# Head-by-head routing of an expert layer: matmul fill moved behind the last head, six mask instructions merged into one, and the row gathers spread

## The chip, the cores and the metric

The kernel runs on one core of a Trainium2 chip. A core has five engines with their own instruction streams: TensorE (PE, matmuls), VectorE (DVE), ScalarE (ACT), GpSimd (POOL) and SyncE (SP, which here only issues DMAs). They meet through semaphores. The metric is device microseconds (us) of one execution, as the median of several runs.

## The reference

One layer of a streaming encoder on 512 tokens of width 1024, in float32. A mixing part (spatial gating and banded attention) is followed by PEER, a layer of 16384 experts, and the change is in PEER's routing:

```
q = (xb @ w_query).reshape(128, 8 heads, 2, 128)
sc = einsum('thpd,hpkd->thpk', q, sub_keys)            # 128 scores for each of the two halves
s_top, i_top = top_k(sc, 16)
cand = s_top[:, :, 0, :, None] + s_top[:, :, 1, None, :]   # 256 sums for each head
best, pos = top_k(cand, 16);  eidx = cand_idx at pos;  g = softmax(best)
h = gelu(einsum('thkd,td->thk', expert_u[eidx], xb))
out = einsum('thkd,thk->td', expert_v[eidx], g * h)
```

So each token chooses 16 experts in each of 8 heads, takes the dot product of its row with 128 rows of `expert_u`, and sums 128 weighted rows of `expert_v`.

## The kernel before

**Dense instead of gathered.** For most tokens the kernel does not gather expert rows. It multiplies all 16384 rows of `expert_u` with the tokens ("first products", 128 tiles of 128 experts, line 553 applies the gelu), builds a matrix of gates from one-hot factors ("one-hot stage", lines 763 to 790), multiplies the two, and multiplies the result with all of `expert_v` ("second product", line 970). Every matmul runs three times on operands split into a high and a low part: `load_split` (lines 119 to 133) loads a tile into one of 3 buffers `raw`, ACT writes `hi` (line 126) and DVE or POOL writes `lo` (line 127), into 5 buffers each. A first-product tile is 24 matmuls into one of two PSUM buffers `pu`, and line 553 on ACT must have read a buffer before the tile after the next may begin.

Two groups of tokens are not dense. Tile 0 (128 tokens) is gathered completely, in the second product's shadow. For the last 64 tokens of tile 3 the dots with `expert_u` are gathered "early": 64 gathers of 128 rows each (two of a token's sixteen experts of a head lie on two partitions, so a head needs 8 gathers), into 6 buffers `rowe`. `indices_early(h)` (lines 501, 502) copies the indices of head h into the tile `eui` on POOL, `gather_early` (line 486) issues indirect DMAs on POOL, `dots_early` (line 495) takes the dots on DVE.

**Routing.** The part of the program from about 225 to 460 us goes head by head. `candidates(h)` splits the head's query weights on POOL, multiplies (48 matmuls into `pa`), copies the result on ACT (line 651, `qt`), multiplies with the keys (line 659), copies the scores (line 662, `scr`) and finds the 16 best keys of each half on DVE (lines 568 to 572). Between these stand first-product tiles as fill for PE: `FILL` tiles in each head, two (`BC`) before head 0, and eight (`BRIDGE`) behind the last head. One iteration later `pairs` adds the keys' scores to 50 candidates (lines 589 to 599) and `choose` takes the 16 best and finds their expert numbers: ACT copies a `tree` (line 606), six bit tests on DVE make masks (line 613), six predicated copies (line 623) select, and line 625 writes `eidx`. I call this the choice of head h, counted from 0 to 7. In each iteration from the third, `indices_early`, then up to six gathers, are queued behind a split on POOL.

After the last choice `indices_of` (lines 677 to 681) makes the digits of the expert numbers, PE transposes them (lines 742, 743), and the one-hot stage begins: 48 steps of 16 small matmuls (line 780), each with a tile `bm` from POOL (line 764) and `am` from DVE (line 772), a quarter of a first-product tile as fill, and gathers for the 64 tokens in the first 33 steps.

**What sets the order.** In routing a list scheduler of the framework decides the order of instructions on each engine from priorities and its own estimates; in the one-hot stage PE, DVE, ACT and POOL follow the order in which the code is written. `tc.issue_after(x)` queues a block's instructions behind x on x's engine. Each engine works through its queue in that order, so an instruction that waits holds all that stand behind it.

## Time and profile before

| | |
|---|---|
| median of three runs | 1463.06 us (1460.8 to 1463.57) |
| the profiled execution: its time, its span | 1460.14 us, 1458.1 us |
| mean granted TensorE clock | 0.986 |
| busy: PEld, ACT, POOL | 1234.7, 615.6, 694.5 us |
| DMA | 396.77 MB, mean 272 GB/s |
| chain that ended last | PE 48%, DVE 9%, DMA 6%, issue 3% |

The page's chain of waits covers the whole program, and the change touches a part of it, so the readings below are of stages: busy time of each engine in a window, and then the instructions that ended PE's idle time. In a row of the timeline the columns are start, duration, engine, line, operation, written tile <- read tiles, shape and count, and in brackets the engine's idle time before it and what ended that. Starts are microseconds from the start of the span.

### The profile page before, as it was taken

The page shows a single profiled execution, that of the slowest core. Times are in us where ns is not written, and L with a number is a line of the kernel's source. Part 1 is how long each engine was busy: PE and PEld are TensorE (multiplying, and loading weights), DVE is VectorE, ACT ScalarE, POOL GpSimd, SP SyncE. Part 2 cuts the span into 40 slices and gives each one's busy share as a digit, 9 for nine tenths or more (in the row PEclk, how much of TensorE's full clock was granted, in tenths as well). Part 3 has the DMA queues.
Part 4 walks back from the last instruction along what each step waited for, and adds up shares of the span by engine and source line. Part 5 has one row for each costly group of instructions (what it writes and reads, how often), then busy time and mean ns, then how long its engine had stood idle before and what let it go on. Part 6 is the DMA issues. An engine that isn't in the chain of part 4 may idle for free.

```text
span 1458.1 us, 21675 instructions
## 1 busy us (share of the span) xinstructions
PE 1397.6 (96%) x7808; PEld 1234.7 (85%) x7808; DVE 1131.7 (78%) x2487; ACT 615.6 (42%) x991; POOL 694.5 (48%) x470
## 2 busy tenths in 40 slices
PE   7999899999988888989999999999999999999998
PEld 5887588888888888979988889989899898888887
DVE  4437643588987887579999999898989889588883
ACT  5447625434344444544444434333433343333331
POOL 0000006478767988605544556555546455244520
PEclk9999999999989999999999999999999999999999
DMA  5352036378656999879889999999999999789981
GB/s 187 116 188 73 17 143 201 110 247 304 219 206 217 296 297 270 259 246 357 309 310 344 328 374 345 359 357 369 384 363 352 361 330 374 273 308 353 332 334 72
DMA packets 164251, 396.77 MB, mean 272 GB/s; under 512 B 12672, under 2 KB 75024, under 8 KB 162096
## 3 DMA queue, kind: packets, MB, share of 16 engines
q1 hardware_dynamic: 65344, 196.76, 37.9%
q0 software_dynamic: 47536, 171.37, 31.9%
q10 hardware_dynamic: 51264, 27.27, 6.4%
q8 instruction: 61, 1.00, 0.3%
q14 instruction: 46, 0.38, 0.1%
HBM read 363.86 MB, written 31.46 MB: 271 GB/s over the span
## 4 chain that ended last, share of the span: by engine, by line
PE 48%; DVE 9%; DMA 6%; issue 3%; ACT 1%; POOL 1%; ACTq 0%; DVEq 0%; POOLq 0%; SPq 0%
PE pa L970 19%; PE px L970 10%; PE pu L144 5%; PE pu L145 5%; PE pu L146 5%; PE pa L780 4%; DVE lo L127 2%; DVE row L911 2%; DMA gd<-gst 2%; DMA sc<-s0d 1%; DMA row<-in_ud,eint 1%; DMA raw<-in_vd 1%; POOL bm L764 1%; DVE acc L922 1%; ACT hi L126 0%
## 5 line engine op out<-in xcount | busy, mean ns | idle before, releaser
L126 ACT ACTIVATE hi<-raw 128x1024 fp32r<-128x1024 f32 x300 | 316.7, 1058 | 469.5 <-DMA raw<-in_vd 137.0
L127 DVE TENSOR_TENSOR lo<-raw,hi 128x1024 fp32r<-128x1024 f32 x248 | 305.1, 1230 | 107.1 <-ACT hi L126 106.0
L909 POOL DMA_INDIRECT row<-in_ud,eint x128 | 201.5, 1574 | 177.8 <-DVE acc L922 121.6
L920 POOL DMA_INDIRECT row<-in_vd,eint x128 | 181.3, 1416 | 172.5 <-DVE row L911 115.6
L144 PE MATMUL pu<-xch,hi 128*128 128x320 f32 x784 | 246.7, 315 | 4.4 <-ACT act L553 4.1
L146 PE MATMUL pu<-xch,lo 128*128 128x320 f32 x784 | 241.3, 308 | 0.3 <-DVE lo L127 0.3
L145 PE MATMUL pu<-xcl,hi 128*128 128x320 f32 x784 | 241.5, 308 | 0.0
L970 PE MATMUL pa<-hi,wh 128*128 128x512 f32 x512 | 200.2, 391 | 0.0
L970 PE MATMUL pa<-lo,wh 128*128 128x512 f32 x512 | 199.6, 390 | 0.0
L127 POOL TENSOR_TENSOR lo<-raw,hi 128x1024 fp32r<-128x1024 f32 x52 | 126.2, 2439 | 88.4 <-ACT hi L126 87.7
L922 DVE SCALAR_TENSOR_TENSOR acc<-row,hw,acc 128x1024 f32<-128x1024 f32 x128 | 164.8, 1288 | 1.2 <-DMA row<-in_vd,eint 1.0
L911 DVE SCALAR_TENSOR_TENSOR row<-row,xb 128x1024 f32<-128x1024 f32 x128 | 157.4, 1232 | 3.9 <-DMA row<-in_ud,eint 3.9
L970 PE MATMUL pa<-hi,wl 128*128 128x512 f32 x512 | 158.3, 389 | 0.0
L144 PEld LDWEIGHTS pu<-xch,hi 128*128 128x128 f32 x784 | 147.6, 188 | 8.4 <-ACT act L553 7.0
L145 PEld LDWEIGHTS pu<-xcl,hi 128*128 128x128 f32 x784 | 147.4, 188 | 1.4
L146 PEld LDWEIGHTS pu<-xch,lo 128*128 128x128 f32 x784 | 147.3, 188 | 0.6 <-DVE lo L127 0.6
L780 PE MATMUL pa<-bm,am 128*128 128x128 f32 x768 | 101.4, 288 | 19.4 <-DVE am L772 11.2
L780 PEld LDWEIGHTS pa<-bm,am 128*128 128x128 f32 x768 | 96.7, 202 | 23.2 <-issue 15.3
L970 PEld LDWEIGHTS pa<-hi,wh 128*128 128x128 f32 x512 | 96.4, 188 | 20.4
L970 PEld LDWEIGHTS pa<-lo,wh 128*128 128x128 f32 x512 | 96.4, 188 | 20.3
L970 PEld LDWEIGHTS pa<-hi,wl 128*128 128x128 f32 x512 | 96.1, 188 | 20.4
L970 PE MATMUL px<-hi,wh 128*128 128x512 f32 x256 | 100.5, 393 | 3.7 <-ACT hi L126 3.7
(215 smaller groups left out, 2618.7 us busy)
## 6 DMA issues: line engine op xcount, KB each, us to landing
raw<-in_uT SPq DMA_DIRECT2D x128, 512.0 KB, 5.6
raw<-in_vd SPq DMA_DIRECT2D x128, 512.0 KB, 5.7
gd<-gst ACTq DMA_DIRECT2D x24, 1024.0 KB, 7.4
gc<-gd SPq DMA_DIRECT2D x15, 1280.0 KB, 8.5
raw<-in_w_in SPq DMA_DIRECT2D x20, 512.0 KB, 4.9
raw<-in_wq SPq DMA_DIRECT2D x16, 512.0 KB, 3.7
raw<-in_w_out SPq DMA_DIRECT2D x8, 512.0 KB, 4.2
gc<-gd SPq DMA_DIRECT2D x15, 256.0 KB, 10.9
```

What stands on the lines that cost most here:

```text
L126: nc.scalar.activation(hi, raw, AF.Copy)
L127: ins = eng.tensor_tensor(lo, raw, hi.bitcast(F32), op=ALU.subtract)
L144: nc.tensor.matmul(ps, lh[0], rh[0], start=first, stop=False)
L145: nc.tensor.matmul(ps, lh[0], rh[1], start=False, stop=False)
L146: nc.tensor.matmul(ps, lh[1], rh[0], start=False, stop=last)
L764: nc.gpsimd.tensor_tensor(bm.rearrange("p t (h l) -> p t h l", l=BL), d[0][:, ts_, :, None].to_broadcast(full), d[1][:, ts_, None, :].to_b ...
L780: nc.tensor.matmul(ps[:, i * P:(i + 1) * P], am[:, 4 * q + i, :], bm[:, 4 * q + i, :], start=True, stop=True)
L909: nc.gpsimd.indirect_dma_start(out=row, out_offset=None, in_=ud, in_offset=bass.IndirectOffsetOnAxis(ap=eint[:, j:j + 1], axis=0))
L911: nc.vector.scalar_tensor_tensor(row, row, 1.0, xb0, op0=ALU.mult, op1=ALU.mult, accum_out=hw[:, j:j + 1])
L920: nc.gpsimd.indirect_dma_start(out=row, out_offset=None, in_=vd, in_offset=bass.IndirectOffsetOnAxis(ap=eint[:, j:j + 1], axis=0))
L922: nc.vector.scalar_tensor_tensor(acc0, row, hw[:, j:j + 1], acc0, op0=ALU.mult, op1=ALU.add)
L970: nc.tensor.matmul(accs[t][half], (wh, wh, wl)[k][:, b, tok], w[b][k % 2][:, ds_], start=first and k == 0, stop=last and k == 2)
```

## The change

- `START` takes the place of `BC` ahead of head 0: one first-product tile where there were two. `FILL` goes from (2, 2, 2, 2, 3, 3, 3, 3) to (1, 1, 1, 3, 3, 3, 3, 3), and `BRIDGE` from 8 to 11. The sum of all three stays 30 tiles. In head 0 the scores stand ahead of the fill tile.
- Six bit tests with a constant become one `tensor_tensor` against a small tile `bits` of six powers of two, over 6 x 48 elements in routing and 6 x 16 where tile 0 is routed later.
- The six gathers of the last head's iteration go: instead one gather follows each of the first six splits of the bridge. `dots_early` is no longer called at the start of the bridge; it is called after the last choice in the code. The index copies for head 6 move from the bridge to behind the last choice, beside those for head 7.
- So 36 gathers are issued by the bridge's end where there were 42, and the one-hot stage asks for a gather in 5 of 6 steps where it was 4 of 6.

```diff
-BRIDGE = 8
+BRIDGE = 11
-FILL = (2, 2, 2, 2, 3, 3, 3, 3)
+START = 1
+FILL = (1, 1, 1, 3, 3, 3, 3, 3)
...
+        bits = const.tile([P, 6], U32, name="bits")
+        for i in range(6):
+            nc.gpsimd.memset(bits[:, i:i + 1], 1 << i)
...
-            for i in range(6):
-                nc.vector.tensor_scalar(mask[:, i * n * TOPK:(i + 1) * n * TOPK], bpos.rearrange("p t k -> p (t k)"),
-                                        1 << i, None, op0=ALU.bitwise_and)
+            full = [P, 6, n * TOPK]
+            nc.vector.tensor_tensor(mask.rearrange("p (l k) -> p l k", l=6),
+                                    bpos.rearrange("p t k -> p (t k)")[:, None, :].to_broadcast(full),
+                                    bits[:, :, None].to_broadcast(full), op=ALU.bitwise_and)
...
-            fill = first_products(sum(FILL[:h]) + BC, FILL[h], nc.gpsimd, True)
-            next(fill, None)
+            fill = first_products(sum(FILL[:h]) + START, FILL[h], nc.gpsimd, True)
+            if h:
+                next(fill, None)
...
         for h in range(NH + 1):
-            dots_early(0)
             if h < NH:
+                dots_early(0)
                 cands.append(candidates(h))
             else:
-                for i, _ in enumerate(first_products(sum(FILL) + BC, BRIDGE, nc.gpsimd, True)):
+                for i, _ in enumerate(first_products(sum(FILL) + START, BRIDGE, nc.gpsimd, True)):
                     behind.append(done[0])
-            if h > 1:
+                    if i < EARLY:
+                        with tc.issue_after(splits[0]):
+                            gather_early(1, gat, ROWA)
+            if 1 < h < NH:
                 with tc.issue_after(splits[0]):
                     indices_early(h - 2)
                     ready_early(h - 2)
-                    gather_early(EARLY, gat, ROWA)
+                    if h < NH - 1:
+                        gather_early(EARLY, gat, ROWA)
...
-        indices_early(NH - 1)
-        ready_early(NH - 1)
+        for h in range(NH - 2, NH):
+            indices_early(h)
+            ready_early(h)
         dots_early(0)
...
-                if n < own - 7 and n % 3 < 2:
+                if n < own - 7 and n % 6 < 5:
                     gather_early(1, gat, ROWA)
```

The rows below show where the instructions stand on their engines, first before and then now. The changed kernel's lines lie 4 to 11 further down the file, so that line 495 is 499 there, and 623 is 628. The first place is DVE at the end of the choice of head 5 (the `eidx` row), before:

```order
L495 SCALAR_TENSOR_TENSOR rowe,du<-rowe,px 128x1024
L623 COPY_PREDICATED tree<-pa,tree 128x48x2
L495 SCALAR_TENSOR_TENSOR rowe,du<-rowe,px 128x1024
L623 COPY_PREDICATED tree<-pa,tree 128x48
L495 SCALAR_TENSOR_TENSOR rowe,du<-rowe,px 128x1024
L625 COPY eidx<-tree 128x3x16
L568 MAX top<-scr 128x8 x2
L569 MAX_INDEX pos<-top,scr 128x8
```

and now:

```order
L628 COPY_PREDICATED tree<-pa,tree 128x48x4
L628 COPY_PREDICATED tree<-pa,tree 128x48x2
L628 COPY_PREDICATED tree<-pa,tree 128x48
L630 COPY eidx<-tree 128x3x16
L499 SCALAR_TENSOR_TENSOR rowe,du<-rowe,px 128x1024
L572 MAX top<-scr 128x8 x2
L573 MAX_INDEX pos<-top,scr 128x8
```

The six dots that stood inside the choice of head 5 are gone from it, and the first dot of the bridge's six gathers stands behind it, ahead of the best keys of head 7. Of the other five, all stand inside the choice of head 6.

The second place is POOL's queue from the index copy for head 4 to the bridge, before:

```order
L501 DMA eui<-eidx 64x8
L502 CAST eui<-eidx 64x8
L127 TENSOR_TENSOR lo<-raw,hi 128x1024 x2
L486 DMA rowe<-in_ud,eui 128x1024 x6
L127 TENSOR_TENSOR lo<-raw,hi 128x1024 x3
L501 DMA eui<-eidx 64x8
L502 CAST eui<-eidx 64x8
L127 TENSOR_TENSOR lo<-raw,hi 128x1024 x5
```

and now:

```order
L505 DMA eui<-eidx 64x8
L506 CAST eui<-eidx 64x8
L131 TENSOR_TENSOR lo<-raw,hi 128x1024 x2
L505 DMA eui<-eidx 64x8
L506 CAST eui<-eidx 64x8
L131 TENSOR_TENSOR lo<-raw,hi 128x1024
L490 DMA rowe<-in_ud,eui 128x1024
L131 TENSOR_TENSOR lo<-raw,hi 128x1024
L490 DMA rowe<-in_ud,eui 128x1024
```

The index copies are for heads 4 and 5. The burst of six gathers between them is gone, and the copy for head 5 stands two splits behind that for head 4. The split behind it is the bridge's first, and the first of the six gathers follows that split.

The third place is DVE in the last choice, before:

```order
L631 TENSOR_TENSOR ex<-gate 128x384
L613 TENSOR_SCALAR pa<-bpos 128x48 x3
L495 SCALAR_TENSOR_TENSOR rowe,du<-rowe,px 128x1024
L613 TENSOR_SCALAR pa<-bpos 128x48 x2
L495 SCALAR_TENSOR_TENSOR rowe,du<-rowe,px 128x1024
L613 TENSOR_SCALAR pa<-bpos 128x48
L623 COPY_PREDICATED tree<-pa,cand 128x48x18
```

and now:

```order
L636 TENSOR_TENSOR ex<-gate 128x384
L617 TENSOR_TENSOR pa<-bpos,bits 128x288
L628 COPY_PREDICATED tree<-pa,cand 128x48x18
L628 COPY_PREDICATED tree<-pa,tree 128x48x16
L628 COPY_PREDICATED tree<-pa,tree 128x48x8
```

No dot stands in the last choice any more.

More of the change, by code (lines that the diff above doesn't have):

```diff
@@ L682, in indices_of @@
             return ff
-        for _ in first_products(0, BC, nc.vector, True):
+        for _ in first_products(0, START, nc.vector, True):
             pass
@@ L713, in hybrid_block @@
         ff = {0: indices_of(GT)}
-        i0 = split = sum(FILL) + BC + BRIDGE
+        i0 = split = sum(FILL) + START + BRIDGE
         def split_next(eng=nc.gpsimd):
```

## The prediction

> **What bounds the kernel now.** I read the page's first part, then the busy times by stage, then what ended PE's idle time in the stage that the change touches.
>
> ```profile
> PE 1397.6 (96%) x7808; PEld 1234.7 (85%) x7808; DVE 1131.7 (78%) x2487; ACT 615.6 (42%) x991; POOL 694.5 (48%) x470
> ```
>
> PE is busy for 96% of the span, and the change leaves the number of matmuls as it is. Only PE's idle time and its clock can be won or lost. The stages below are the first heads, the later heads, bridge and last choice, the gathering part of the one-hot stage, and the second product; the columns are span, PE, PEld, DVE, ACT and POOL busy, then granted clock, DMA share and GB/s.
>
> ```profile
> 225.00:285.00 60.00, 59.20 (x327) 53.38 (x328) 24.43 (x143) 26.87 (x46) 34.42 (x14) 0.97 0.52 163
> 285.00:413.00 128.00, 125.06 (x730) 113.85 (x728) 116.93 (x534) 52.10 (x97) 98.69 (x72) 1.00 0.73 256
> 413.00:466.00 53.00, 42.62 (x257) 41.87 (x258) 39.93 (x167) 21.44 (x32) 34.12 (x25) 0.90 0.54 181
> 466.00:570.00 104.00, 91.18 (x689) 88.08 (x689) 84.70 (x107) 44.21 (x78) 93.58 (x57) 0.95 0.96 294
> 625.00:1458.00 833.00, 823.78 (x4320) 728.73 (x4320) 713.50 (x1246) 326.56 (x469) 393.25 (x265) 1.00 0.88 328
> ```
>
> DVE is idle for 36 of the first 60 us and then busy for 117 of 128: it starts late and runs behind. PE pays at the end, with 10.4 us of idle time in the 53 us of bridge and last choice, and a clock of 0.90. The second product has PE at 99%, so the mask saving there is worth nothing. PE's rows with idle time from the bridge to the first one-hot product:
>
> ```profile
> 415.75 0.63 PE L144 MATMUL pu<-xbh,hi 128*128 128x320 f32 x1 [2.79 <-ACT act L553]
> 424.68 0.41 PE L144 MATMUL pu<-xbh,hi 128*128 128x320 f32 x1 [2.35 <-ACT act L553]
> 457.76 0.55 PE L742 MATMUL pa<-ident,ii 128*128 128x128 f32 x3 [3.13 <-ACT ii L681]
> 465.85 3.30 PE L780 MATMUL pa<-bm,am 128*128 128x128 f32 x16 [2.15 <-issue]
> ```
>
> ACT and DVE show what held the two `act`:
>
> ```profile
> 414.31 1.06 ACT L126 ACTIVATE hi<-raw 128x1024 fp32r<-128x1024 f32 x1 [6.88 <-DMA raw<-in_uT]
> 422.81 1.48 ACT L606 COPY tree<-cand 128x1536 f32<-128x1536 f32 x1 [7.12 <-DVE cand L599]
> 421.75 0.25 DVE L599 TENSOR_TENSOR cand<-top,pa 128x96 f32<-128x96 f32 x1
> 443.89 1.22 DVE L495 SCALAR_TENSOR_TENSOR rowe<-rowe,px 128x1024 f32<-128x1024 f32 x1 [3.99 <-DMA rowe<-in_ud,eui]
> ```
>
> The first `act` stood behind a `hi` whose tile came late. The second stood behind the `tree` copy of head 6, which waited for DVE's candidates. The third gap is the last choice, in which DVE waited 3.99 us for a gather. So DVE's progress through the choices sets the bridge.
>
> **The change part by part.** I take the choice of head 5 (its `eidx` row) as the mark, since the order after it stays the same up to PE's restart.
>
> First the fill. A tile's time is the distance from the first of its 24 matmuls to the next block, and a head's query product that of its 48:
>
> ```profile
> 236.70 0.39 PE L144 MATMUL pa<-xbh,hi 128*128 128x512 f32 x1
> 247.60 0.30 PE L144 MATMUL pu<-xbh,hi 128*128 128x320 f32 x1
> 251.12 1.95 PE L659 MATMUL pa<-skt,qt 128*128 128x128 f32 x16
> ```
>
> A tile is 3.5 us and a query product 10.9. Ahead of the scores of head 1 stood five tiles and now stand three; two tiles are 7.0 us, and I take 6.5, as the scores of head 0 now follow their query product with only four matmuls between and may wait for the copy. Later heads' scores come earlier still (head 3 by four tiles), so PE no longer holds DVE there. What DVE did between the choices:
>
> ```profile
> 272.73 0.49 DVE L568 MAX8 top<-scr 128x8 f32<-128x128 f32 x2 [12.35 <-ACT scr L662]
> 289.19 0.24 DVE L625 COPY eidx<-tree 128x48 f32<-128x48 f32 x1
> 393.77 0.22 DVE L625 COPY eidx<-tree 128x48 f32<-128x48 f32 x1
> 415.05 0.24 DVE L625 COPY eidx<-tree 128x48 f32<-128x48 f32 x1
> 431.71 0.24 DVE L625 COPY eidx<-tree 128x48 f32<-128x48 f32 x1
> L495 DVE SCALAR_TENSOR_TENSOR rowe<-rowe,px 128x1024 f32<-128x1024 f32 x36 | 43.9, 1219 | 6.9 <-DMA rowe<-in_ud,eui 6.5
> L568 DVE MAX8 top<-scr 128x8 f32<-128x128 f32 x36 | 9.9, 282 | 3.0 <-ACT scr L662 3.0
> ```
>
> The `eidx` rows are the choices of heads 0, 4, 5 and 6; the last two rows group 285 to 425 us. From choice 4 to 5 passed 21.3 us with six dots inside, from 5 to 6 16.7 us with none, so a dot costs 0.8 us there (it fills gaps between dependent instructions).
>
> The masks:
>
> ```profile
> L613 DVE TENSOR_SCALAR pa<-bpos 128x48 uint32<-128x48 uint32 x48 | 10.0, 208 | 1.0
> 458.51 0.42 DVE L753 TENSOR_TENSOR hb<-iota_k,pa 128x256 f32<-128x256 f32 x1 [1.35 <-POOL eui L502]
> ```
>
> Six of 208 ns are 1.25 us, with their gaps about 1.45. The merged one has 288 elements, which no row shows; between the 0.42 us of 256 broadcast elements and that of 512 (twice as much) I take 0.45, as it is nearest to the first. It saves 1.0 us a choice (0.6 at worst).
>
> Choice 0 then ends at 289.2 - 6.5 - 1.0 = 281.7. From choice 0 to 5 passed 125.9 us. I take off the 3.0 us wait for scores, the 6.5 us of waits for gathers, five masks (5.0) and seven dots (30 stand there now, 37 before; 5.6), and get 105.8. New waits for gathers come on top. In the changed order POOL's gathers stand in smaller pieces between splits (2.4 us each), and I laid the two queues side by side with the prices of the next fence: 2.0 us in choice 1, 2.7 in choice 3, 2.0 in choice 4, 0.4 elsewhere, 7.1 in all. The bounds are none and the 9.5 that stood there before. Choice 5 falls at 281.7 + 105.8 + 7.1 = 394.6 (387.5 to 397), 20.5 us earlier than now.
>
> Then the new wait. DVE's next instruction is the first dot of the bridge's gathers, and on POOL that gather stands behind the index copy that waits for this very choice, and behind a split:
>
> ```profile
> 415.58 0.56 POOL L501 DMA_DIRECT2D eui<-eidx  x1 [1.09 <-DVE top L568]
> 416.46 2.37 POOL L127 TENSOR_TENSOR lo<-raw,hi 128x1024 fp32r<-128x1024 f32 x1
> DMA to landing us min/median/max: 5.8/5.9/7.1
> ```
>
> From the `eidx` at 415.05 to the end of the copies at 416.46 are 1.4 us, the split is 2.4, and a gather lands 5.9 us after its issue (the third row, of the seven gathers from 430 to 460 us): 9.7, and 1.2 for the dot itself. Thus DVE starts head 7's keys 10.9 us later than it could. Behind the dot stand these keys and the candidates of head 6; for the candidates waits ACT's `tree`, for that the `act` behind it, and for that PE, whose second bridge tile needs the buffer.
>
> The Trainium skill, "DMA: Bandwidth & Descriptors", section "Anatomy of one DMA", gives a GpSimd-issued DMA about 2.0 us and its bytes at 436 GB/s, by which a gather of 512 KB would land after an estimated 3.2 us and the sum would come out 2.7 us lower. The trace says 5.9 and decides.
>
> From the `eidx` of choice 5 to PE's restart passed 424.68 - 415.05 = 9.6 us before. Now PE restarts at 394.6 + 10.9 + 9.6 = 415.1, although its own work would bring it there at about 402. Behind it lie eleven tiles to the transposes (ten of the bridge, one held back) where there were eight: 38.7 us, against 28.2. On the half clock: of the 53 us the clock missed 10%, that is 5.3 us, some of it on the tile ahead of a wait where it cost nothing. 424.68 + 28.2 + 1.7 gives 454.6, which is where the gap at 457.76 begins, so 1.7 was paid behind the restart; after a stall of 13 us I allow 1.7 to 3.4. The transposes come at 455.5 to 457.2. The last choice is over long before, so its 3.1 us of waiting go. Against 457.76 that is a gain of 0.6 to 2.3; I take 1.5.
>
> Last the six gathers, which are not saved but moved into the one-hot stage. POOL's groups from 460 to 570 us, two of PE's rows there, and the gathers' queue and their issues in a view of 480 to 580 us:
>
> ```profile
> L764 POOL TENSOR_TENSOR bm<-hb,lb 128x1024 f32<-128x1024 f32 x34 | 65.5, 1938 | 5.8 <-PE pa L780 3.2 <-DVE lb L753 2.3
> L486 POOL DMA_INDIRECT rowe<-in_ud,eui x21 | 23.3, 1108 | 3.3 <-issue 2.4 <-DVE lb L753 0.2 <-DVE am L772 0.2
> L127 POOL TENSOR_TENSOR lo<-raw,hi 128x1024 fp32r<-128x1024 f32 x4 | 9.6, 2395 | 4.6 <-ACT hi L126 4.6
> 494.32 2.05 PE L780 MATMUL pa<-bm,am 128*128 128x128 f32 x16 [1.41 <-POOL bm L764]
> 503.84 3.65 PE L780 MATMUL pa<-bm,am 128*128 128x128 f32 x16 [3.50 <-DVE am L772]
> q0 software_dynamic: 2639, 9.50, 29.7%
> rowe<-in_ud,eui POOLq DMA_INDIRECT x17, 6.6
> ```
>
> Six gathers of 1.11 us with 0.16 us of issue are 7.6 us more for a POOL that is busy for 93.6 of 104. Its slack, 3.2 us of waiting for PE and 4.6 for `hi`, could swallow them, so the lower bound is nothing. The upper is 10: the 17 gathers issued in those 100 us took 29.7% of the DMA engines, 1.7 us each, while the share stood at 0.96. POOL ends few of PE's gaps (1.41 us), DVE the larger (3.50), so I take 2.5. The six dots more (1.3 us each) lie in DVE's 19 idle us.
>
> The sum is 1460.1 - 1.5 + 2.5 = 1461.1 for the profiled execution. Its runs' median lies 2.9 above it, which gives 1464.0, no change.
>
> **The rivals.** The first is that the gathers hold DVE less than I say. With no wait in choices 1 to 4, choice 5 falls at 387.5 and the transposes 7.1 us earlier: 1456.9. If DVE reached its dot only after the gather had landed, 10.9 us would go, and 1453 is the end of that case. For it speaks that the waits were laid out by hand; against it, that the first gather cannot be issued before choice 5 is over, wherever that falls.
>
> The second ends slower: the one-hot stage pays the gathers in full. POOL becomes the engine that each step waits for once the 7.8 us of its waits are used up, or the DMA engines do at a share that can't rise; the price is 7.6 to 10, and the time 1463.1 - 1.5 + 7.6 to 10, thus 1469 to 1472. For it speaks POOL's 90% and the DMA's 0.96, against it that DVE's waits there leave POOL time.
>
> A third is that the change does all that its description says, the dots behind the last choice, no wait for a gather: 20.5 + 3.1 - 10.5 earlier, 13 us and so 1452 with the gathers' 2.5. The order of DVE speaks against it, so it has little weight and counts with the first.
>
> **How the numbers follow.** About 0.2%, 2.9 us, is what a measurement of this kernel can tell from no change. No change has a chance of 0.37, the first rival with the third 0.33, the second 0.30. The likeliest case's own range is 1460.2 to 1466; to hold eight in ten I go to 1454.5 and 1470.5, into both rivals.
>
> **What would show it.** Right would be: choice 5 at 394 us, a DVE wait of about 9 us for `rowe` right behind it, PE idle for 10 to 13 us in the bridge until 415, and transposes that wait for nothing at 456. Choice 5 after 400, or the transposes before 450, would make the first part wrong. In the one-hot stage, a first product to thirty-third step that takes over 5 us longer would make the second rival right, a length within 1 us my 2.5 too high. PE waiting for `lo` in heads 3 to 7 would mean that POOL, which I take as hidden there, binds.

## The result, and the profile after

The changed kernel takes 1477.6 us (median of four runs, 1474.9 to 1481.9), the kernel before 1461.9 beside it: a ratio of 1.0112 with a 95% interval of 1.0082 to 1.0142. It is slower by 16 us, and 13.6 us above the forecast. The profiled execution took 1474.91 us with a span of 1473.1.

Busy times by stage, first of the kernel before and then of the changed one. The first row of each is routing up to the first one-hot product, the second the one-hot stage up to the first matmul of the second product. The columns are span, PE, PEld, DVE, ACT and POOL busy, granted clock, DMA share and GB/s.

```profile
225.00:465.85 240.85, 226.73 (x1313) 208.95 (x1313) 181.14 (x842) 100.41 (x174) 167.08 (x110) 0.97 0.64 216
465.85:625.27 159.42, 138.42 (x1057) 134.31 (x1057) 118.31 (x150) 72.45 (x126) 127.46 (x78) 0.96 0.92 275
```

```profile
225.00:470.59 245.59, 225.73 (x1307) 207.18 (x1306) 184.13 (x789) 99.79 (x173) 162.70 (x105) 0.97 0.61 200
470.59:641.53 170.94, 141.24 (x1057) 136.46 (x1057) 130.36 (x162) 72.37 (x126) 134.41 (x84) 0.94 0.89 275
```

Routing is 4.7 us longer and the one-hot stage 11.5; the second product, from there to the end of the span, is 1.2 us shorter (831.6 against 832.8). The second rows also say how the 11.5 us are made up: PE's idle time (span less busy) went from 21.0 to 29.7 us, and PE needed 2.8 us more for the same matmuls, at a clock of 0.94 instead of 0.96.

PE's rows with long idle times, of the changed kernel, from the bridge to the second product:

```profile
408.92 0.42 PE L148 MATMUL pu<-xbh,hi 128*128 128x320 f32 x1 [2.75 <-ACT act L557]
420.20 0.63 PE L148 MATMUL pu<-xbh,hi 128*128 128x320 f32 x1 [5.96 <-ACT act L557]
462.55 0.49 PE L753 MATMUL pa<-ident,ii 128*128 128x128 f32 x3
584.95 3.43 PE L791 MATMUL pa<-bm,am 128*128 128x128 f32 x16 [3.39 <-DVE am L783]
595.87 3.76 PE L791 MATMUL pa<-bm,am 128*128 128x128 f32 x16 [4.83 <-DVE am L783]
616.88 2.02 PE L791 MATMUL pa<-bm,am 128*128 128x128 f32 x16 [2.03 <-DVE am L783]
```

The restart in the bridge comes at 420.2 us, five later than forecast, and the transposes (line 753) wait for nothing, as forecast, but at 462.6 instead of 456. The other three rows are in the one-hot stage. They show the clock as well: the same 16 matmuls took 2.02 us behind a wait of 2.03, 3.43 behind 3.39 and 3.76 behind 4.83, and the granted clock in these three stretches was 1.00, 0.57 and 0.50.

On DVE stand the marks of the prediction: the choices of heads 0, 5 and 6, and the first dot behind choice 5. The last row groups all 36 dots from 225 to 470 us.

```profile
281.13 0.23 DVE L630 COPY eidx<-tree 128x48 f32<-128x48 f32 x1
400.10 0.24 DVE L630 COPY eidx<-tree 128x48 f32<-128x48 f32 x1
409.56 1.22 DVE L499 SCALAR_TENSOR_TENSOR rowe<-rowe,px 128x1024 f32<-128x1024 f32 x1 [9.22 <-DMA rowe<-in_ud,eui]
435.26 0.24 DVE L630 COPY eidx<-tree 128x48 f32<-128x48 f32 x1
L499 DVE SCALAR_TENSOR_TENSOR rowe<-rowe,px 128x1024 f32<-128x1024 f32 x36 | 43.7, 1214 | 15.9 <-DMA rowe<-in_ud,eui 15.9
```

Choice 0 is where it was forecast (281.7), choice 5 is 5.5 us late (forecast 394.6). What is late between them is the instruction that was to save time, the merged mask. Its group, two of its rows, and POOL's row beside the first of them:

```profile
L617 DVE TENSOR_TENSOR pa<-bpos,bits 128x288 uint32<-128x288 uint32 x8 | 18.1, 2262 | 0.3
297.85 6.20 DVE L617 TENSOR_TENSOR pa<-bpos,bits 128x288 uint32<-128x288 uint32 x1
324.22 0.46 DVE L617 TENSOR_TENSOR pa<-bpos,bits 128x288 uint32<-128x288 uint32 x1
```

```profile
296.60 7.12 POOL L131 TENSOR_TENSOR lo<-raw,hi 128x1024 fp32r<-128x1024 f32 x3
```

The eight masks of routing took 18.1 us, where 48 bit tests had taken 10.0. Three of the eight took 0.46 to 0.49 us, which is the price that was forecast; the other five took 2.2 to 6.2. The longest began while POOL was in three splits that end at 303.72 and ended at 304.05, 0.33 us behind them. The other four long ones also ended 0.3 us behind the end of one of POOL's splits; the three short ones fell where POOL was issuing gathers (one began 0.2 us before a split's end). Both operands of the mask, `bpos` and `bits`, lie in SBUF (the on-chip memory of the tiles, as against PSUM, the buffers into which PE's matmuls write), and so do both operands of POOL's split. The Trainium skill, "SBUF — State Buffer", section "Who interferes with whom", says that a DVE instruction with two SBUF inputs contends with a GpSimd instruction that reads SBUF; the rows agree, with 0.46 us where POOL had no split and up to 6.20 behind three splits. The bit tests had one SBUF operand and a constant, wrote to PSUM, and never took over 0.213 us.

### The profile page after: what moved, and what is told of

Same layout as the page of the kernel before. It is cut to its first block, busy times and chain, and to the rows that moved or that the text cites. A ratio compares the mean times of both kernels' runs of the same rounds, so it can differ in the third digit from the quotient of the medians.

```text
span 1473.1 us, 21606 instructions
## 1 busy us (share of the span) xinstructions
PE 1399.8 (95%) x7808; PEld 1237.6 (84%) x7808; DVE 1145.0 (78%) x2406; ACT 616.5 (42%) x991; POOL 700.1 (48%) x477
## 4 chain that ended last, share of the span: by engine, by line
PE 54%; DVE 9%; issue 3%; DMA 2%; ACT 1%; POOL 1%; ACTq 0%; DVEq 0%; POOLq 0%
PE pa L981 20%; PE px L981 10%; PE pu L148 6%; PE pu L150 6%; PE pu L149 6%; PE pa L791 4%; DVE lo L131 2%; DVE row L922 2%; DMA gd<-gst 1%; DVE acc L933 1%; DMA sc<-s0d 1%; DVE am L783 1%; POOL bm L775 1%; DMA rowe<-in_ud,eui 1%; DVE ii L685 0%
## 5 line engine op out<-in xcount | busy, mean ns | idle before, releaser
L131 POOL TENSOR_TENSOR lo<-raw,hi 128x1024 fp32r<-128x1024 f32 x53 | 129.3, 2455 | 80.4 <-ACT rstd L156 40.6
```

Of the source, the lines that this page charges most:

```text
L131: ins = eng.tensor_tensor(lo, raw, hi.bitcast(F32), op=ALU.subtract)
```

## Experiments

All ratios below are to the kernel before, run beside on the same chip, with a 95% interval. Stage lengths are those of each kernel's profiled execution, cut as above; where that execution lies far from its kernel's median, the text says so.

**Routing: the mask.** The changed kernel, with the powers of two copied by ACT into six free columns of the mask's PSUM buffer:

```diff
+                powers = ps[:, 8 * ND * TOPK:8 * ND * TOPK + 6].bitcast(U32)
+                nc.scalar.copy(powers, bits)
...
-                                    bits[:, :, None].to_broadcast(full), op=ALU.bitwise_and)
+                                    powers[:, :, None].to_broadcast(full), op=ALU.bitwise_and)
```

> The changed kernel, with one operand of the merged mask moved: ACT copies the six powers of two into six free columns of the PSUM buffer in which the mask lies, and DVE reads them there. Theory: the merged mask (eight times in routing, 2.37 us on the mean, 6.20 us the longest) is long because DVE reads two SBUF tiles in it, and so stands until a split on POOL is over. Then all eight take 0.4 to 0.55 us here, choice 1 ends some 5 us earlier, choice 5 at 391 to 396 us instead of 400.1 (gathers that land late take some of it back), PE restarts in the bridge at 411 to 416, and the run takes 1466 to 1471 us where the changed kernel's profiled run took 1474.9. Rival: 288 elements simply cost that much (or the time is something else's that the profile books here): the eight stay at 2.4 us on the mean and the time within 1 us of the changed kernel's.

(The 2.37 us in it is the median of the eight; the mean is 2.26.) It took 1468.8 us, ratio 1.0051 (1.0032 to 1.0069). The masks of routing, choice 5 and the restart:

```profile
L617 DVE TENSOR_TENSOR pa<-bpos,pa 128x288 uint32<-128x288 uint32 x8 | 3.7, 457 | 0.2
391.99 0.24 DVE L630 COPY eidx<-tree 128x48 f32<-128x48 f32 x1
411.78 0.64 PE L148 MATMUL pu<-xbh,hi 128*128 128x320 f32 x1 [6.96 <-ACT act L557]
```

The same 288 elements cost 0.457 us each with one operand in PSUM. Choice 5 comes 8.1 us earlier, PE's restart 8.4, the first one-hot product 8.6 (462.0). The matmuls, and DVE's order up to choice 4, are those of the changed kernel; ACT has eight small copies more. The rival falls: the length was not the mask's own.

The kernel before with the merged mask alone, both operands in SBUF:

> The kernel before with the merged mask alone, both operands in SBUF (the scheduler moves some gathers and dots with it). Theory of the port: in a choice POOL splits more than half of the time, so the eight masks take 1.5 to 3 us each on the mean where six bit tests took 1.45 with their gaps; the choices come later and the run takes 1464 to 1470 us against 1462. Rival (the prediction's price, 0.45 us each and 1.0 saved in every choice): 1457 to 1462 us.

1467.2 us, ratio 1.0044 (1.0021 to 1.0067): slower, as the theory has it. Its profiled execution lies 14 us above its median, so only the instruction's length is read from it:

```profile
L617 DVE TENSOR_TENSOR pa<-bpos,bits 128x288 uint32<-128x288 uint32 x8 | 15.1, 1888 | 0.3
```

**Routing: the dot behind choice 5.** The changed kernel with the bridge's dots really behind the last choice:

```diff
...
-        dots_early(0)
+        with tc.issue_after(last):
+            dots_early(0)
         routing.close()
```

(`last` is the `eidx` copy that `choose` now returns.)

> The changed kernel, with the dots of the bridge's six gathers queued on DVE behind the last choice, where the code has them and the scheduler did not put them. Theory (the prediction's step on the new wait): the wait of 9.2 us for the first of these gathers, and its dot, hold the keys of head 7, and through them ACT's tree and PE's restart, by 10.9 us. Without them choice 6 comes at 424 to 426 us instead of 435.3, PE restarts at about 410 instead of 420.2, the gaps of 2.75 and 5.96 us shrink by 6 at least, and the run takes 1465 to 1468 us. Rival: something else is as late (ACT's splits, whose tiles land late, or the last choice), PE restarts at 415 or later and the time falls by less than 3 us.

1473.8 us, ratio 1.0074 (1.0048 to 1.0099), some 4 to 6 us better than the changed kernel, though the two intervals overlap. The choices of heads 5 and 6 lie 19.2 us apart instead of 35.2, but PE gained far less. PE's gaps, its routing stage, and what held the first `act`:

```profile
411.57 0.42 PE L148 MATMUL pu<-xbh,hi 128*128 128x320 f32 x1 [1.26 <-ACT act L557]
429.20 0.42 PE L148 MATMUL pu<-xbh,hi 128*128 128x320 f32 x1 [2.11 <-ACT act L557]
225.00:468.17 243.17, 227.71 (x1317) 208.02 (x1317) 187.19 (x790) 100.82 (x174) 164.75 (x105) 0.98 0.61 204
```

```profile
410.13 1.06 ACT L130 ACTIVATE hi<-raw 128x1024 fp32r<-128x1024 f32 x1 [5.70 <-POOL lo L131]
```

Of 8.7 us of gaps 3.4 are left, and PE's idle time from 225 us to the first one-hot product fell from 19.9 to 15.5. From choice 5 to the first product pass 65.5 us instead of 70.5 (the stage as a whole is only 2.4 us shorter, as choice 0 came 2.4 us later in this execution). So the wait of 10.7 us on DVE was worth 4 to 5 us to PE: behind it stand the bridge's tiles, which come from POOL's splits and from loads. The result falls between my two theories.

**The fill alone**, with the six bit tests and the gathers of before:

> The kernel before with the change's fill alone (one tile ahead, fill moved from the first heads behind the last, scores of head 0 ahead of its fill tile), six bit tests, gathers as before. Theory (the prediction's step on the fill): choice 0 ends 6 to 8 us earlier (281 to 283 us), the choices behind it keep most of that, no dot is bound to a gather that waits for choice 5, and the run takes 1456 to 1460 us. Rival: the lead is given back in DVE's waits for gathers and in PE's bridge; the first one-hot product comes at 464 to 467 us as before and the run takes 1460 to 1463.

1456.7 us, ratio 0.9949 (0.9922 to 0.9977): faster. Choice 0 came at 281.48 us and the first one-hot product at 463.4; the one-hot stage took 162.0 us, 2.6 more than before, in an execution that lies 1.4 us above its median, and the second product 2.3 less. So the trace shows 2.5 us gained in routing and given back in the one-hot stage; where the rest of the gain between the runs' medians lies, it does not show.

**The gathers alone** on the kernel before, with old fill and bit tests (of the change's diff, the parts that move the gathers and the index copies and set the pace in the one-hot stage):

> The kernel before with the gathers' part of the change alone: no burst of six in the last head's iteration, one behind each of the bridge's first six splits, 5 of 6 steps in the one-hot stage; six bit tests and the old fill. Theory: most of the one-hot stage's loss comes with it, since the gathers make POOL and DVE late there, and the tail and DVE's instructions with two SBUF operands pay for that: first to last product plus rest 166 to 171 us against 159.4, the routing stage within 3 us of before, the run 1467 to 1475. Rival: the one-hot stage loses by the late start or by the merge, and stays within 2 us of 159.4 here; then the run takes 1460 to 1465.

1474.0 us, ratio 1.0092 (1.0066 to 1.0118). Its one-hot stage, in an execution 7 us below its median:

```profile
465.04:634.64 169.60, 140.77 (x1056) 136.16 (x1057) 129.56 (x162) 72.25 (x126) 134.09 (x84) 0.94 0.90 277
```

10.2 us more than before, and routing within 1 us. So the three parts alone are, by their ratios, worth +13 us (gathers), +6 (merged mask) and -7 (fill), 12 in sum; the whole change is +16 with an interval of 12 to 21.

**The one-hot stage: where its 11.5 us went.** I took the start of the first matmul of each of the 48 steps, counted from the first product. The changed kernel is 2.2 us behind the kernel before at the thirty-third step, 4.2 at the next, 9.0 at the thirty-sixth, and 11.5 from the thirty-seventh to the end. So most is lost where the dots have to be finished. Two rows of DVE and two of POOL of the changed kernel there:

```profile
582.09 1.22 DVE L499 SCALAR_TENSOR_TENSOR rowe<-rowe,px 128x1024 f32<-128x1024 f32 x1 [4.00 <-DMA rowe<-in_ud,eui]
589.84 4.64 DVE L520 TENSOR_TENSOR gate<-gate,dots 64x128 f32<-64x128 f32 x1 [2.52 <-ACT dots L519]
```

```profile
574.20 0.99 POOL L490 DMA_INDIRECT rowe<-in_ud,eui  x1 [0.16 <-issue]
588.61 5.70 POOL L775 TENSOR_TENSOR bm<-hb,lb 128x1024 f32<-128x1024 f32 x3
```

At 5 steps of 6 the last gather is issued at 574.2, one step ahead of the place where all dots are taken, and DVE stands 4.0 us for its rows. Then the early dots are multiplied into the gates, 64 x 128 elements with two SBUF operands; that took 0.79 us before, and 4.64 here, ending 0.17 us behind three of POOL's tiles. Two runs change one of these each. The multiplication from PSUM:

```diff
-                nc.scalar.activation(dots[own], dots[own], AF.Gelu_apprx_tanh)
+                nc.scalar.activation(xbu[own, 0:NH * TOPK], dots[own].rearrange("p a b k -> p (a b k)"), AF.Gelu_apprx_tanh)
```

> The changed kernel, with ACT writing the gelu of the early dots into a PSUM buffer that is free by then, from which DVE multiplies it into the gates (64 x 128 elements). Theory: that multiplication took 4.64 us in the changed kernel and 0.79 before, since both its operands lie in SBUF and POOL wrote three one-hot tiles without a pause. Here it takes 0.3 to 0.5 us, PE's wait of 4.83 us for the next one-hot factor behind it shrinks to about 1, and the time is 1470.5 to 1472 us against 1474.9. Rival: PE waits there for something else that is as late (the copies of the dots and the gelu), and the time stays within 1 us.

1473.1 us, ratio 1.0079 (1.0050 to 1.0107); the stage took 166.8 us, 4.2 less. The stage gained what the theory says, but the run lies just above its range, its interval overlaps that of the changed kernel, and PE now waited longer elsewhere for a one-hot factor (4.58 us at one place). The instruction:

```profile
L520 DVE TENSOR_TENSOR gate<-gate,px 64x128 f32<-64x128 f32 x1 | 0.3, 291 | 2.2 <-ACT px L519 2.2
```

The last gather earlier:

```diff
-                if n < own - 7 and n % 6 < 5:
+                if n < own - 12:
```

> The changed kernel, with the 28 gathers of the one-hot stage issued in its first 28 steps, one in each, instead of in 28 of the first 33. Theory: 10.3 of the stage's 11.5 us were lost from step 33 to 37, of which 4.0 us are DVE waiting for the last gather, which was issued one step ahead of the place where all dots have to be done. Here it is issued five steps earlier: that wait goes, steps 33 to 37 lose about 6 us against the kernel before instead of 10.3, the denser first part costs 1 to 2, and the time is 1471 to 1473 us. Rival (the second of the prediction: the six gathers' time on POOL or on the DMA engines is paid wherever they stand): the first 33 steps get longer by what the end gains, and the time stays within 1 us of 1475.

1478.3 us, ratio 1.0108 (1.0064 to 1.0152), no gain, and the rival's reading is not enough either. The wait of 4.0 us was gone, but two instructions stood behind POOL's tiles for longer than in the changed kernel (rows of DVE and POOL):

```profile
563.63 6.41 DVE L685 TENSOR_SCALAR ii<-ei 128x128 int32<-128x128 int32 x1
592.53 6.05 DVE L520 TENSOR_TENSOR gate<-gate,dots 64x128 f32<-64x128 f32 x1 [1.12 <-ACT dots L519]
```

```profile
564.25 5.69 POOL L775 TENSOR_TENSOR bm<-hb,lb 128x1024 f32<-128x1024 f32 x3
592.73 5.69 POOL L775 TENSOR_TENSOR bm<-hb,lb 128x1024 f32<-128x1024 f32 x3
```

The first is the middle shift of the digits, which has one tensor operand and a target, both in SBUF; it takes 0.2 us when POOL pauses. The same section of the Trainium skill counts `tensor_scalar` among the instructions that can, with suitable operands, use two ports of SBUF and so contend with GpSimd; these rows agree. The kernel before had the same stall, beside two of POOL's tiles and ahead of the wait of 3.50 us for `am` that the prediction shows at 503.84:

```profile
497.91 4.53 DVE L679 TENSOR_SCALAR ii<-ei 128x128 int32<-128x128 int32 x1
498.52 3.81 POOL L764 TENSOR_TENSOR bm<-hb,lb 128x1024 f32<-128x1024 f32 x2
```

So I took all three kinds (masks, gates, digits) off SBUF pairs, that is, gave each an operand in PSUM: the masks and the gates as in the two runs above, the digits by copying the expert numbers into PSUM ahead of the shifts:

```diff
-            ei = gat.tile([P, NH * TOPK], I32, name="ei", tag="ei", bufs=1)
+            ei = pa()[:, 0:NH * TOPK].bitcast(I32)
```

> The changed kernel with the three kinds of DVE instruction that were found long moved off two SBUF operands: the powers of two and the gelu of the dots in PSUM as before, and the copy of the expert numbers from which the digits are shifted in PSUM too. Theory: the digits' second shift took 3.59 us on the mean in the one-hot stage (0.23 for the others) because POOL was writing one-hot tiles, 6 to 7 us in two; with it and the gates' 4.6 gone, the one-hot stage takes 161 to 165 us instead of 170.9, the routing gain of the powers in PSUM (8.6 us) stays, and the run takes 1459 to 1464. Rival (the six gathers' own time on POOL and the DMA engines is the cost): the stage stays above 167 us and the run above 1465.

1462.8 us, ratio 0.9997 (0.9965 to 1.0030): the changed kernel without these stalls is no slower than the one before. The shifts took 0.28 to 0.29 us each. But the stage stayed at 166.0 us, between the theory and its rival. The same with the gathers as before the change:

> The kernel before with the change's fill and merged mask, the three kinds of instruction off two SBUF operands as in the run above, and the gathers as before the change (a burst of six, 4 of 6 steps). Theory: routing gains what the powers in PSUM gave there (first one-hot product at 460 to 463 us instead of 465.9), the one-hot stage 2 to 4 us on top (157 instead of 159.4), and the run takes 1453 to 1458 us, faster than both kernels. Rival: the fill is worth something only together with the gathers spread over the bridge, and the run takes 1459 us or more.

1454.4 us, ratio 0.9967 (0.9945 to 0.9989), faster than both kernels. And the kernel before with the merged mask and the three kinds moved, so without the fill:

> The kernel before with the merged mask and the three kinds of instruction off two SBUF operands, old fill, old gathers: the run of the fill with all that (1454.4 us) less the fill. Theory: the one-hot stage is shorter than before here too (155 to 157 us instead of 159.4), the routing about as before (464 to 466), and the run takes 1456 to 1460. Rival: all of that run's gain came from the fill, and the run takes 1461 us or more.

1456.0 us, ratio 0.9963 (0.9931 to 0.9994), with a first product at 465.2 and a one-hot stage of 154.7 us, as the theory has it: that run's gain did not all come from the fill. With it the first product came 3.1 us earlier, but the two runs' ratios are the same within their intervals.

The runs with all three kinds moved differ in the gathers alone, 166.0 us with the change's and 154.7 with those of before, from first products at 462.20 and 462.18. That is the cost of six gathers moved, 11.3 us in the stage, without the stalls on masks, gates and digits; the runs' medians lie 8.4 us apart. Three runs take it apart. Without six of the 28 dots:

```diff
+        SKIP = (40, 45, 50, 55, 60, 63)
...
                 j, row = issued.pop(0)
+                if j in SKIP:
+                    continue
```

> The changed kernel with the three kinds of instruction off two SBUF operands (1462.8 us, one-hot stage 166.0 us against 154.7 where the gathers are as before), less six of the 28 dots of the one-hot stage, every fifth and the last; their gathers are still issued. It leaves out six of the 64 early rows' dot products. Theory: what the six moved gathers cost is paid on DVE, in dots, their waits and the splits and one-hot factors that stand behind them, so the stage takes 154 to 159 us and the run 1451 to 1456. Rival (the prediction's second): it is paid on POOL and the DMA engines, which here do as much as there; the stage stays at 163 to 166 us and the run at 1460 to 1463.

1463.0 us, ratio 0.9987 (0.9958 to 1.0017), no gain: the rival. (The stage of its profiled execution, 172.0 us, counts little, as that lies 7 us above the median; there one split on DVE stood 5.5 us.) Without the six gathers, all 28 dots kept (six of them on a row that is already there):

```diff
+        SKIP = (40, 45, 50, 55, 60, 63)
...
+                if j in SKIP:
+                    issued.append((j, issued[-1][1]))
+                    continue
                 row = rows_of.tile([P, D], F32, name="rowe", tag="rowe", bufs=n_rows)
```

> The changed kernel off two SBUF operands (1462.8 us, one-hot stage 166.0 us), less six of the one-hot stage's 28 gathers, every fifth and the last; DVE still takes 28 dots, six of them on the row of the dot before. It leaves out six of the 64 early rows' dot products. If POOL's and the DMA engines' time for the gathers is the cost, the stage takes 153 to 158 us; if DVE's dots are, it stays at 163 to 167 us.

1451.8 us, ratio 0.9917 (0.9885 to 0.9949). With POOL's time kept and the transfers dropped:

```diff
-                nc.gpsimd.indirect_dma_start(out=row, out_offset=None, in_=ud,
...
+                if j in SKIP:
+                    nc.gpsimd.memset(row, 0.0)
+                else:
+                    nc.gpsimd.indirect_dma_start(out=row, out_offset=None, in_=ud,
...
```

> The changed kernel off two SBUF operands (one-hot stage 166.0 us; 153.4 without six gathers), with the same six gathers replaced by a memset of the same row tile on POOL (128 x 1024, some 1 us). It leaves out six of the 64 early rows' dot products (they come out as zero). If POOL's time is the cost, the stage takes 162 to 166 us where a memset is as long as a gather's issue (1.11 us), 2 us less for each 0.2 us by which it is shorter. If the transfers are the cost, it takes 153 to 157 us.

1455.0 us, ratio 0.9940 (0.9908 to 0.9971). The one-hot stages of three kernels: 28 gathers, 22 gathers, 22 gathers and six memsets; then the memsets' group.

```profile
462.20:628.21 166.01, 139.61 (x1057) 135.12 (x1057) 124.51 (x162) 72.38 (x126) 133.09 (x84) 0.94 0.92 282
```

```profile
462.30:615.69 153.39, 134.37 (x1057) 129.28 (x1057) 120.59 (x162) 72.84 (x126) 127.91 (x78) 0.98 0.94 285
```

```profile
460.99:617.76 156.77, 136.40 (x1057) 130.85 (x1057) 121.45 (x162) 73.19 (x126) 132.69 (x84) 0.97 0.93 279
L492 POOL MEMSET rowe<- 128x1024 f32 x6 | 5.8, 962 | 0.0
```

Six gathers cost 12.6 us: 7.4 of idle time on PE (26.4 against 19.0), and 5.2 because the same matmuls ran at a clock of 0.94 instead of 0.98. POOL's time is the smaller part: 5.8 us of memsets cost 3.4 (a memset takes 0.96 us, a gather's issue 1.11, so this is a little too small). The other 9.2 come with the transfers and what waits for them. Each length is of one execution, and the intervals of the runs with memsets and without them overlap, so the division is rough. By the starts of the steps, 4.5 of the 9.2 are lost from the thirty-third step to the thirty-fifth, where DVE again waits for the last gather's rows, 3.2 from the forty-second to the forty-fourth, where one of DVE's own splits took 2.87 us, and the rest before. So the last gather counts. Moved ahead, with everything off SBUF pairs:

> The changed kernel off two SBUF operands, with one gather in each of the first 28 steps, so that the last is issued five steps ahead of the end. If the late last gather is a cost of its own (from step 33 to 34 the stage lost 4.3 us), the stage takes 161 to 163 us; if POOL pays for each gather wherever it stands, the first 28 steps get longer by as much and it stays at 165 to 168 us.

The stage took 163.5 us, 2.5 less than 166.0, but 5.0 were lost by the thirty-third step and the run took 1464.3 us, ratio 1.0017 (0.9995 to 1.0040), no better than with 5 of 6 steps. The last gather's wait and the earlier loss both show, and the sum is nothing.

Last, the splits of the one-hot stage on DVE alone, with the change's gathers and with those of before:

```diff
-                    split_next(nc.vector if split % 2 else nc.gpsimd)
+                    split_next(nc.vector)
```

> The changed kernel off two SBUF operands, with all splits of the one-hot stage on DVE, where every other one was on POOL (five at 2.4 us there, 1.2 to 3.3 us here). If POOL is what the stage waits for, its 12 us go and the stage takes 156 to 162 us instead of 166.0. If DVE is, five more splits stand in its way, each as long as POOL's tiles hold it, and the stage takes 168 us or more.

> The run of the fill off two SBUF operands (1454.4 us, one-hot stage 154.7 us, gathers as before the change), with all splits of the one-hot stage on DVE. If POOL binds there too, the stage takes 148 to 152 us and the run 1448 to 1452, faster than both kernels. If DVE's queue binds, the stage takes 156 us or more.

1471.2 us (ratio 1.0050, 1.0021 to 1.0080) and 1467.5 (1.0038, 1.0017 to 1.0059), both slower than without this edit. The first one's stage, 164.2 us in an execution 4 us below its median, fits neither theory as it stands: two splits now stand on DVE ahead of the first one-hot factors, where one stood, so the stage begins 3.7 us later, and the second product starts at 630.0 instead of 628.2. The second's is clear, 166.1 against 154.7, from a start some 4 us later too. DVE's splits from 462 to 625 us in the second:

```profile
L132 DVE TENSOR_TENSOR lo<-raw,hi 128x1024 fp32r<-128x1024 f32 x11 | 23.9, 2176 | 21.6 <-ACT hi L131 21.6
```

A split on DVE holds its queue twice, for ACT's `hi` (21.6 us in all, 10.3 without this edit) and for POOL's tiles (2.18 us on the mean, where the shortest take 1.21). POOL is not what the stage waits for alone.

**Better versions.** With the fill and everything off SBUF pairs, I queued the six dots that stood behind choice 5 behind choice 6:

```diff
         for h in range(NH + 1):
-            dots_early(0)
+            with tc.issue_after(last) if h == NH else ExitStack():
+                dots_early(0)
```

> The run of the fill with all instructions off two SBUF operands (1454.4 us; PE waited 12.57 us in one gap of its bridge), with the six dots that stood right behind choice 5 queued behind choice 6. Theory: they hold head 7's keys, so choice 6 comes 10 to 12 us earlier (411 to 413 us instead of 422.8), PE's gap of 12.57 us falls below 4, the first one-hot product comes at 453 to 457 us instead of 462.2 and the run takes 1446 to 1450 us. Rival: the dots only move the delay to the last choice, whose digits the transposes wait for, and the gain stays under 3 us.

1457.7 us, ratio 0.9958 (0.9925 to 0.9991), not better than without. In an execution 6 us below its median, choice 6 came at 414.7 us instead of 422.8, PE's gap stayed, and its reason is on ACT:

```profile
409.12 0.64 PE L149 MATMUL pu<-xbh,hi 128*128 128x320 f32 x1 [12.27 <-ACT act L557]
```

```profile
407.69 1.06 ACT L131 ACTIVATE hi<-raw 128x1024 fp32r<-128x1024 f32 x1 [12.77 <-DMA raw<-in_uT]
```

The tile's load was late, as in the run without this edit (a wait of 13.10 us at the same place), so there the dots had not held PE, and the rival's reason (the last choice) was wrong too. Fill as in the change, bit tests and gathers of before, with gates and digits off SBUF pairs:

> The kernel before with the change's fill, its own six bit tests and gathers, and the digits' and the gates' instructions of the one-hot stage off two SBUF operands. If the parts add up (fill alone: first product at 463.4 us; the one-hot stage off two SBUF operands: 154.7), the run takes 1448 to 1452 us, faster than both kernels. If they don't, it takes 1455 us or more like the fill alone (1456.7).

1451.1 us, ratio 0.9911 (0.9880 to 0.9942), faster than both kernels, and the parts add up: first product at 462.4, one-hot stage 155.3. It has six bit tests; the same with the merged mask in PSUM took 1454.4.

## Why the prediction was wrong, step by step

It foresaw 1464.0 us, no change, with 1470.5 as its upper end; 1477.6 lies above. In the profiled execution it expected routing to gain 1.5 us and the one-hot stage to lose 2.5; routing lost 4.7 and the stage 11.5.

- **PE bounds, and the mask is worth nothing in the second product**: no saving showed there. In this pair that stage changed by 1.2 us, but over all profiled executions it took 830.4 to 832.9 us in the four kernels with six bit tests (831.5 on the mean) and 831.6 to 836.2 in the sixteen with the merged mask (834.3). The masks in it took 0.29 us at most, so why it is longer stays open.
- **The fill** was right in its place: choice 0 at 281.1 against 281.7, though its mask took 2.23 us instead of 0.45. That it came so close is partly luck: the 6.5 us of earlier scores were some 2.4 too few here (1.2 in the run with the fill alone, where choice 0 came 7.7 us earlier). Alone the fill gains 7 us by its ratio, 5 by the medians.
- **"The merged one ... I take 0.45 ... It saves 1.0 us a choice (0.6 at worst)"** is the first step that failed. I bounded the cost by the element count of other rows and asked nothing about what POOL does meanwhile, though a DVE row of 4.53 us beside POOL's tiles stood in the trace of the kernel before. The masks of choices 1 to 5 took 10.1 us (6.20, 0.46, 0.49, 0.48, 2.50) where 2.25 were forecast. Less 1.7 for DVE's waits for gathers, 5.4 us (15.9 less 9.22, 0.57 and 0.69 behind choice 5) against 7.1, that is 6.2, and choice 5 fell 6.1 us further behind choice 0 than forecast, at 400.1, just past the 400 that I had named as the sign of a wrong first part. With the operand in PSUM choice 5 came at 392.0 and the first product 3.9 us ahead of the kernel before: with that price right, routing would have gained 2.4 us more than I said.
- **The new wait, 10.9 us**: from the `eidx` at 400.1 to the dot's end passed 10.7. **9.6 us to the restart**: 9.4 from the dot's end to 420.2. **Eleven tiles and half clock, 40.4 to 42.1**: 42.4 to the transposes, which waited for nothing. These held, the last just above its bound. That PE's "own work" would bring it to its restart 13 us earlier did not hold: PE's two gaps come to 8.7 us, not 10 to 13, and without the dots they shrink by 5 us, and tiles that come late take the dots' place.
- **"Six gathers ... so I take 2.5"** is the second step that failed. The threshold that I set, first product to thirty-third step, came out at 2.2, as forecast, but it stopped short of the loss: 9.3 us were lost in the four steps behind. I had counted POOL's time and the DMA engines' share, and laid the dots into DVE's idle time. I had also read PE's wait of 3.50 us for `am` as DVE's alone, while the row that made DVE late, the digits' shift, stood behind POOL's tiles. And I had not asked when the last gather would be issued. At 5 of 6 steps it comes one step ahead of the place where all dots must be taken. DVE waited for it for 4.0 us, then 4.64 us at the gates' multiplication, behind POOL's tiles, and PE stood. The second rival (the gathers paid in full) had the sign, and its price of 7.6 to 10 lay just under the 10.2 to 12.6 that the runs show for them; it was paid less on POOL (3.4) than it said. It also left out the clock, 5.2 of 12.6 us in the pair of runs that measures it.
- **The first rival and the third** (faster) did not come out: DVE waited 9.2 us behind choice 5, and the dots stood inside the choice of head 6. Times near theirs (1454 and 1451 us) came by another way, with the fill, the gathers as before and operands in PSUM.

Still open is how the 9.2 us that came with the transfers divide between waits for landing rows and DVE's splits that happen to fall on POOL's tiles; moving the last gather forward brought no gain, and neither did leaving out six dots.

## What to carry to other kernels

Before six small instructions are merged into one, look at where the new operands lie and what the neighbour engine does at that time: here a DVE instruction with two SBUF operands took up to 13 times its length beside a busy POOL (6.20 us against 0.46), and copying six numbers into PSUM removed that. Look in the old trace for short instructions of the same engine that take long with no wait in front of them. When work is moved into a stage that looks idle enough, find the place where it must be finished and see what is issued last, since the stage's average says nothing of it. And price a stall on PE with the slower matmuls that follow it.

## What the hardware showed that was not expected

- A DVE instruction that meets POOL's tiles does not get in between two of them for certain: three shown above lasted until three POOL instructions in a row had ended (6.20 us behind splits, 6.41 and 6.05 behind one-hot tiles), for work of 0.2 to 0.8 us.
- The clock lost nearly as much as the idle time in the pair with and without six gathers: 5.2 and 7.4 us, and the same 16 matmuls took 2.02 us behind a wait of 2.03 and 3.76 behind one of 4.83.
- DVE's own splits, whose operands are both in SBUF, took 1.2 to 5.5 us in the one-hot stage even where masks, gates and digits had been moved. Three of their rows, of the runs with 28 gathers, with six memsets, and without six dots:

```profile
597.90 2.87 DVE L131 TENSOR_TENSOR lo<-raw,hi 128x1024 fp32r<-128x1024 f32 x1 [2.09 <-ACT hi L130]
```

```profile
590.54 1.23 DVE L131 TENSOR_TENSOR lo<-raw,hi 128x1024 fp32r<-128x1024 f32 x1 [1.90 <-ACT hi L130]
```

```profile
556.51 5.52 DVE L131 TENSOR_TENSOR lo<-raw,hi 128x1024 fp32r<-128x1024 f32 x1
```
